# Attention core on TensorE: transposes, scores and values pinned in written order, with lags of six and nine steps instead of five and eight

## The chip, the cores and the metric

The kernel runs on one core of a Trainium2 chip. The metric is the device time of one execution in microseconds (us). The kernel before was timed in three runs; its median is 1542.38 us.

## The reference, cut to what matters

The program is one step of a two-layer trunk over 128 context tokens and 512 latent tokens, width 1024. Layer 0 is a convolution beside an mLSTM, layer 1 is grouped-query attention; each is followed by a SwiGLU feed-forward (FFN). The change lies in layer 1, in the attention of the latent tokens: 8 query heads of width 128, 2 key/value heads, 640 keys (512 latent and 128 cached).

```python
q, k, v = qkv_proj(h, w_in, qg, kg)          # per-head RMSNorm of q and k
q, k = rope_2d(q), rope_2d(k)
k_all = jnp.concatenate([k, k_ctx], axis=1)  # 512 + 128 keys
v_all = jnp.concatenate([v, v_ctx], axis=1)
o = blocked_attention(q, k_all, v_all)       # softmax(q k^T * scale) v, per head
return o @ w_out
```

The 128 context tokens attend only to themselves, in a small computation of their own.

## The kernel before, in words

**Arithmetic.** A product of high precision is made of three matmuls in a rounded float32 form. Each operand is split into a high and a low part, and `mm3` (line 200) issues high×high (line 204), high×low (205) and low×high (206). The splits are made on ScalarE (high part), and on VectorE or GpSimd (low part): line 112 and 115 for weights, 510 and 511 for results (`split_to`).

**Order of the work.** The program is traced by Python in the order in which it is written, and a scheduler then chooses each engine's order: it runs a simulation of the program, and where the next instruction in written order isn't ready there, a later one that is ready goes first. What it chose is fixed in the program; on the chip each engine works through its own list. `issue_after` and `keep_in_program_order` add an edge that the scheduler must respect: the second puts an instruction behind the one that was traced just before it on the same engine. It orders two instructions of one engine and waits for nothing else.

**The attention core.** `attn_layer` (1375) projects keys and values, then queries in two halves (`qc` 0 and 1, five token blocks each, `proj_B`). The core is a generator, `core` (1551), of numbered steps g. Step g works on head g // 5. For g % 5 in 0 to 3 it scores one block of 128 queries against 640 keys (`score`, 1503): two times three matmuls of 320 columns into a pair of PSUM banks (`p2`, two of them), then on VectorE a maximum over the row (1514) and its scaling (1515), on ScalarE the exponential with its sum (1517), on VectorE the reciprocal (1519), on GpSimd the normalisation (1520). The fourth block's result lies in a tile "t", the others in a tile "pw".

A number of steps TL later, step g transposes one block of 128 keys of a head's four probability blocks (`trans`, 1522; TensorE, line 1525, four transposes into one PSUM bank `p1`, of which there are four). The result is copied to a tile "h" as high part (ScalarE, 1532; for the fourth key block VectorE, 1530) and low part (VectorE, 1534). A number of steps VL later, `value` (1536) multiplies it with the values into one more `p1` bank, held over the head's five key blocks: three matmuls of 512 columns (1545 to 1547), or for the cached block one float32 product that runs as two matmuls (1543). After the fifth, `split_to` writes the head's output into H2.

Within a step the written order is transposes, scores, values, and in some steps the transposes of late query blocks (`put_q`, 1451, line 1454) or a piece of the context's attention (`context`, 1466, lines 1470, 1483, 1488).

Nine steps are taken between the blocks of the second query projection. The rest follow in `attn_layer`'s last loop, which hands H2 to `out_proj` (527) ten steps ahead of the end; `out_proj` issues 18 matmuls of heads 0 to 5 ahead of each of the next four steps, takes the remaining steps in a row, and goes on with heads 6 and 7 and the other output tiles.

Of the kernel before, what the change touches and what calls it, by code (L numbers as in the profile page):

```python
# [13 lines left out]
P = 128  # L14
# [32 lines left out]
class Kern:  # L47
# [149 lines left out]
    def p2(self):  # L197
        return self.psp.tile([P, 2, 512], F32, tag="p2", name="p2", bufs=self.pairs)

    def mm3(self, out, w, x, first, last):  # L200

        t = self.nc.tensor
        with self.behind(self.then):
            t.matmul(out, w[0], x[0], start=first, stop=False)  # L204
        t.matmul(out, w[0], x[1], start=False, stop=False)  # L205
        t.matmul(out, w[1], x[0], start=False, stop=last)  # L206

# [1167 lines left out]
    def attn_layer(self, H, mods):  # L1375


        nc, I = self.nc, self.I
# [5 lines left out]
        V, Vl = [self.ht(FR)[:, :1024].rearrange("p (k n) -> p k n", k=4) for _ in range(2)]  # L1384
# [26 lines left out]
        V4 = [self.st()[:, :P] for _ in range(2)]  # L1411
# [49 lines left out]
        def rcol(hq, t, i):  # L1461
            o = 4 * t + hq % 4
            return rk[:, hq // 4, i, o:o + 1]


        def context(kv):
            p = self.p1()
            for i in range(4):
                hq = kv * 4 + i
                nc.tensor.matmul(p[:, i * P:(i + 1) * P], qT[hq // 2][:, hq % 2, 0:P], kTc[:, kv],  # L1470
                                 start=True, stop=True)
            mx, sm, Pm = self.col(4), self.col(4), self.tt()[:, :512].rearrange("p (h n) -> p h n", h=4)
            nc.vector.tensor_reduce(mx, p.rearrange("p (h n) -> p h n", h=4), AX.X, ALU.max)
            nc.vector.tensor_tensor(mx, mx, rk[:, kv, 1, 0:4], ALU.mult)
            for i in range(4):
                nc.scalar.activation(Pm[:, i], p[:, i * P:(i + 1) * P], AF.Exp, bias=mx[:, i:i + 1],
                                     scale=rcol(kv * 4 + i, 0, 0), accum_out=sm[:, i:i + 1])
            nc.vector.reciprocal(sm, sm)
            nc.gpsimd.tensor_tensor(Pm, Pm, sm.unsqueeze(2).to_broadcast([P, 4, P]), ALU.mult)
            yield  # L1480
            pt = self.p1()
            for i in range(4):
                nc.tensor.transpose(pt[:, i * P:(i + 1) * P], Pm[:, i], self.ident)
            PT = self.tt()[:, :512]
            nc.vector.tensor_copy(PT, pt)
            yield
            po = self.p1()
            nc.tensor.matmul(po, Vc[kv], PT, start=True, stop=True)
            self.split_to(H2[:, kv * 4:kv * 4 + 4, 0, 0:P], H2[:, kv * 4:kv * 4 + 4, 1, 0:P],
                          po.rearrange("p (h n) -> p h n", h=4))  # L1490


        Q, Ps, PT, po = {}, {}, {}, {}
        projected = []

        def query(hq):
            Q[hq] = self.ht(FR)
            src = qT[hq // 2][:, hq % 2, P:TOK]
            hi, lo = Q[hq][:, 0:512], Q[hq][:, 640:1152]
            nc.scalar.activation(hi, src, AF.Copy)  # L1500
            nc.gpsimd.tensor_tensor(lo, src, hi.bitcast(F32), ALU.subtract)

        def score(hq, t):
            kv, q = hq // 4, Q[hq]
            if t == 0:
                w = self.wtile(name="pw")
                Ps[hq] = [w[:, i * TOK:(i + 1) * TOK] for i in range(3)] + [self.tt()[:, :TOK]]
            pa = self.p2()[:, :, :HF]
            for a in range(2):
                self.mm3(pa[:, a], (q[:, t * P:(t + 1) * P], q[:, 640 + t * P:640 + (t + 1) * P]),  # L1510
                         (kT[kv][:, a * HF:(a + 1) * HF], kT[kv][:, TOK + a * HF:TOK + (a + 1) * HF]),
                         True, True)
            mx, sm = self.col(1), self.col(1)
            nc.vector.tensor_reduce(mx, pa, AX.XY, ALU.max)
            nc.vector.tensor_scalar(mx, mx, rcol(hq, t + 1, 1), None, ALU.mult)
            Pm = Ps[hq][t]
            nc.scalar.activation(Pm.rearrange("p (a n) -> p a n", a=2), pa, AF.Exp, bias=mx,
                                 scale=rcol(hq, t + 1, 0), accum_out=sm)
            nc.vector.reciprocal(sm, sm)
            nc.gpsimd.tensor_scalar(Pm, Pm, sm[:, 0:1], 0.0, ALU.mult, ALU.add)  # L1520

        def trans(hq, kt):
            p = self.p1()
            for t in range(4):
                nc.tensor.transpose(p[:, t * P:(t + 1) * P], Ps[hq][t][:, kt * P:(kt + 1) * P], self.ident)  # L1525
            h = self.ht(F32 if kt == 4 else FR)
            hi, lo = h[:, :512], h[:, 640:1152]
            PT[hq, kt] = hi, lo
            if kt in (3,):
                nc.vector.tensor_copy(hi, p)  # L1530
            else:
                nc.scalar.activation(hi, p, AF.Copy)
            if kt < 4:
                nc.vector.tensor_tensor(lo, p, hi.bitcast(F32), ALU.subtract)

        def value(hq, kt):
            kv = hq // 4
            if kt == 0:
                po[hq] = self.p1()
            sl = slice(kv * P, (kv + 1) * P)  # L1540
            hi, lo = PT.pop((hq, kt))
            if kt == 4:
                nc.tensor.matmul(po[hq], V4[kv], hi, start=(kt == 0), stop=(kt == 4))
            else:
                nc.tensor.matmul(po[hq], V[:, kt, sl], hi, start=(kt == 0), stop=False)  # L1545
                nc.tensor.matmul(po[hq], Vl[:, kt, sl], hi, start=False, stop=False)
                nc.tensor.matmul(po[hq], V[:, kt, sl], lo, start=False, stop=(kt == 4))
            if kt == 4:
                self.split_to(H2[:, hq, 0, P:TOK], H2[:, hq, 1, P:TOK], po.pop(hq))

        def core():
            query(0)
            TL, VL = 5, 8
            for g in range(40 + VL):
                yield g
                if g > 11:
                    self.wcap = 3
                if TL <= g < 40 + TL:
                    trans((g - TL) // 5, (g - TL) % 5)
                hq, t = g // 5, g % 5  # L1560
                if hq < 8:
                    if t < 4:
                        score(hq, t)
                    else:
                        self.tick(1, 10)
                    if t == 2 and hq < 7:
                        query(hq + 1)
                if VL <= g < 40 + VL:
                    value((g - VL) // 5, (g - VL) % 5)
                if projected and late and g % 3 == 2:  # L1570
                    late.pop(0)()
                if g in (8, 18):
                    ctx = context(g // 10)
                if g in (9, 13, 16, 19, 23, 26):
                    next(ctx, None)

        steps = core()
        for qc in range(2):
            if qc == 1:
# [30 lines left out]
            self.wdone(4)  # L1610
        projected.append(1)
        for g in steps:
            if g >= 30 + 8:
                yield H2
        self.wcap = 6
        yield
# [316 lines left out]
```

## Time and profile before

| What | Value |
|---|---|
| Median of 3 runs | 1542.38 us (1541.84 to 1544.18) |
| The profiled execution's own time | 1540.22 us |
| Its span in the trace | 1538.4 us |
| TensorE busy (matmuls) | 1509.1 us, 98% of the span |
| VectorE, ScalarE, GpSimd busy | 905.8, 582.7, 539.9 us |
| Mean granted TensorE clock | 0.998 of full speed |

A row of a timeline gives start, duration, engine, line, operation and tiles, and in brackets the idle time of the engine before it with what ended it. Matmuls are pipelined: the duration of one reaches to its modelled end, and the next may start earlier; what one costs is the distance from its start to the next start. PEld is the load of a matmul's stationary operand.

### The profile page before, as it was taken

To read this page: it belongs to the slowest core of one execution; us is meant where nothing else is said; L and a number is where in the kernel's file an instruction comes from. 1 tells how busy PE (TensorE), PEld (TensorE's weight loads), DVE (VectorE), ACT (ScalarE), POOL (GpSimd) and SP (SyncE) were. 2 spreads that over 40 slices of the span, in tenths; PEclk is the share of its full clock that TensorE was granted. 3 is DMA by queue.
4 is the path that set the end of the run, shared out by engine and by line. 5 is a ranking of instruction groups with operands and counts; after the bars stand their busy time and mean duration, and the time that the engine had idled before them with its cause. 6 is when DMAs were issued, how large, how long until landed. Compare 5 with 4: busy or idle time off the path is not lost.

```text
span 1538.4 us, 24266 instructions
## 1 busy us (share of the span) xinstructions
PE 1509.1 (98%) x9722; PEld 1405.2 (91%) x9722; DVE 905.8 (59%) x1514; ACT 582.7 (38%) x1153; POOL 539.9 (35%) x366
## 2 busy tenths in 40 slices
PE   8899999999999999999999999999999999999998
PEld 7789888899999999999998877899998998989996
DVE  5888633668976773756576588747653333333335
ACT  5666558444212212212135448626431221212123
POOL 3388411232213222222232445423325524344341
PEclk9999999999999999999999999999999999999999
DMA  9323223534534342423353121122321221312121
GB/s 366 125 87 113 93 90 110 189 124 134 181 110 144 112 156 83 137 75 132 101 177 120 42 82 37 42 102 83 118 102 55 83 83 41 110 55 98 67 69 69
DMA packets 63850, 165.36 MB, mean 107 GB/s; under 512 B 6904, under 2 KB 14112, under 8 KB 63738
## 3 DMA queue, kind: packets, MB, share of 16 engines
q1 hardware_dynamic: 63050, 162.90, 31.0%
q8 instruction: 76, 1.25, 0.3%
q10 hardware_dynamic: 688, 0.92, 0.2%
q14 instruction: 36, 0.29, 0.1%
HBM read 157.53 MB, written 6.26 MB: 106 GB/s over the span
## 4 chain that ended last, share of the span: by engine, by line
PE 84%; DVE 6%; DMA 3%; ACT 3%; POOL 1%; issue 1%; SPq 0%; ACTq 0%; DVEq 0%; POOLq 0%
PE p L204 25%; PE p L206 25%; PE p L205 25%; PE p L263 1%; ACT w L112 1%; POOL w L115 1%; PE p L1525 1%; DVE acc L236 1%; DMA raw<-in_wab 1%; DMA raw<-in_wfo 1%; DVE w L115 1%; PE p L1545 1%; DVE h L524 1%; DVE acc L234 1%; POOL t L903 1%
## 5 line engine op out<-in xcount | busy, mean ns | idle before, releaser
L204 PE MATMUL p<-H,w 128*128 128x320 f32 (+1 forms) x1968 | 609.7, 311 | 3.6 <-ACT t L869 2.2
L206 PE MATMUL p<-H,w 128*128 128x320 f32 (+1 forms) x1968 | 608.8, 310 | 0.0
L205 PE MATMUL p<-H,w 128*128 128x320 f32 (+1 forms) x1968 | 607.1, 309 | 0.0
L115 POOL TENSOR_TENSOR w<-raw,w 128x1024 fp32r<-128x1024 f32 x123 | 310.4, 2528 | 729.8 <-ACT w L112 714.4
L204 PEld LDWEIGHTS p<-H,w 128*128 128x128 f32 x1968 | 369.8, 188 | 13.6 <-issue 3.4
L205 PEld LDWEIGHTS p<-H,w 128*128 128x128 f32 x1968 | 370.5, 188 | 0.7 <-issue 0.2
L206 PEld LDWEIGHTS p<-H,w 128*128 128x128 f32 x1968 | 370.0, 188 | 1.3 <-issue 1.1
L112 ACT ACTIVATE w<-raw 128x1024 fp32r<-128x1024 f32 x178 | 186.9, 1057 | 385.2 <-PE p L206 259.0
L236 DVE SCALAR_TENSOR_TENSOR acc<-mraw,cs,acc 128x512 f32<-128x512 f32 x196 | 174.8, 937 | 0.0
L1629 DVE TENSOR_TENSOR t<-t,p 128x320 f32<-128x320 f32 x88 | 42.6, 484 | 178.4 <-ACT t L1628 176.6
L1628 ACT ACTIVATE t<-p 128x320 f32<-128x320 f32 x88 | 38.1, 433 | 215.3 <-PE p L206 215.3
L115 DVE TENSOR_TENSOR w<-raw,w 128x1024 fp32r<-128x1024 f32 x55 | 77.2, 1404 | 63.0 <-ACT w L112 63.0
L204 PE MATMUL p<-h,w 128*128 128x320 f32 x352 | 109.3, 310 | 1.2 <-DVE h L524 1.2
L511 DVE TENSOR_TENSOR h<-t,h 128x320 fp32r<-128x320 f32 x88 | 87.4, 993 | 36.1 <-ACT h L510 36.1
L205 PE MATMUL p<-h,w 128*128 128x320 f32 x352 | 108.6, 309 | 0.0
L206 PE MATMUL p<-h,w 128*128 128x320 f32 x352 | 108.6, 309 | 0.0
L524 DVE SCALAR_TENSOR_TENSOR h<-p,modT,h 128x128 f32<-128x128 f32 (+2 forms) x189 | 75.0, 431 | 56.5 <-PE p L206 56.4
L517 DVE TENSOR_TENSOR t<-p,h 128x512 f32<-128x512 f32 (+1 forms) x61 | 41.4, 681 | 80.8 <-PE p L206 80.2
L205 PE MATMUL p<-w,h 128*128 128x512 f32 (+1 forms) x224 | 87.9, 392 | 0.0
L204 PE MATMUL p<-w,h 128*128 128x512 f32 (+1 forms) x224 | 87.8, 392 | 0.0
L518 POOL TENSOR_TENSOR h<-h,t 128x512 f32<-128x512 f32 x50 | 69.4, 1391 | 52.0 <-DVE t L517 52.0
L206 PE MATMUL p<-w,h 128*128 128x512 f32 (+1 forms) x224 | 87.6, 391 | 0.0
(346 smaller groups left out, 2150.3 us busy)
## 6 DMA issues: line engine op xcount, KB each, us to landing
raw<-in_wfi SPq DMA_DIRECT2D x88, 512.0 KB, 3.5
mraw<-in_wmod SPq DMA_DIRECT2D x160, 256.0 KB, 3.4
raw<-in_wfo SPq DMA_DIRECT2D x44, 512.0 KB, 3.5
raw<-in_wab SPq DMA_DIRECT2D x16, 512.0 KB, 3.5
raw<-in_wc SPq DMA_DIRECT2D x12, 512.0 KB, 3.9
h<-in_xT SPq DMA_DIRECT2D x14, 320.0 KB, 6.1
h<-in_wmod SPq DMA_DIRECT2D x8, 512.0 KB
raw<-in_woab SPq DMA_DIRECT2D x8, 512.0 KB, 3.5
```

The source lines that it names most:

```text
L112: self.hi_last = self.nc.scalar.activation(hi, r, AF.Copy).ins,
L115: e.tensor_tensor(lo, r, hi.bitcast(F32), ALU.subtract)
L204: t.matmul(out, w[0], x[0], start=first, stop=False)
L205: t.matmul(out, w[0], x[1], start=False, stop=False)
L206: t.matmul(out, w[1], x[0], start=False, stop=last)
L236: nc.vector.scalar_tensor_tensor(acc[:, c], w, s, bias if k == 0 else acc[:, c], ALU.mult, ALU.add)
L511: j = self.nc.vector.tensor_tensor(lo, src, hi.bitcast(F32), ALU.subtract)
L517: nc.vector.tensor_tensor(tmp, ps, gate, ALU.mult)
L518: (e or nc.gpsimd).tensor_tensor(x, x, tmp, ALU.add)
L524: self.nc.vector.scalar_tensor_tensor(x, ps[:, b - a * HF:e - a * HF], gate[:, k, c:c + 1], x, ALU.mult, ALU.add)
L1628: nc.scalar.activation(s[:, sl], pg, AF.Silu)
L1629: nc.vector.tensor_tensor(s[:, sl], s[:, sl], pu, ALU.mult)
```

## The change

It adds edges of the kind `keep_in_program_order` to the first matmul of each group of the core: the first of a `score` (its first half alone), the first of the four transposes of a `trans`, the first matmul of a `value`. Transposes come six steps behind the scores (TL 6, it was 5) and values nine (VL 9, it was 8); the core has 49 steps instead of 48, and H2 is handed over at step 39 instead of 38. The start and stop flags in `value` are written as constants of the same value.

```diff
-    def mm3(self, out, w, x, first, last):
+    def mm3(self, out, w, x, first, last, pin=False):
...
         with self.behind(self.then):
-            t.matmul(out, w[0], x[0], start=first, stop=False)
+            i = t.matmul(out, w[0], x[0], start=first, stop=False)
+        if pin:
+            self.tc.keep_in_program_order(i)
         t.matmul(out, w[0], x[1], start=False, stop=False)
...
                 self.mm3(pa[:, a], (q[:, t * P:(t + 1) * P], q[:, 640 + t * P:640 + (t + 1) * P]),
                          (kT[kv][:, a * HF:(a + 1) * HF], kT[kv][:, TOK + a * HF:TOK + (a + 1) * HF]),
-                         True, True)
+                         True, True, a == 0)
...
             for t in range(4):
-                nc.tensor.transpose(p[:, t * P:(t + 1) * P], Ps[hq][t][:, kt * P:(kt + 1) * P], self.ident)
+                i = nc.tensor.transpose(p[:, t * P:(t + 1) * P], Ps[hq][t][:, kt * P:(kt + 1) * P], self.ident)
+                if t == 0:
+                    self.tc.keep_in_program_order(i)
...
             if kt == 4:
-                nc.tensor.matmul(po[hq], V4[kv], hi, start=(kt == 0), stop=(kt == 4))
+                self.tc.keep_in_program_order(nc.tensor.matmul(po[hq], V4[kv], hi, start=False, stop=True))
             else:
-                nc.tensor.matmul(po[hq], V[:, kt, sl], hi, start=(kt == 0), stop=False)
+                self.tc.keep_in_program_order(
+                    nc.tensor.matmul(po[hq], V[:, kt, sl], hi, start=(kt == 0), stop=False))
                 nc.tensor.matmul(po[hq], Vl[:, kt, sl], hi, start=False, stop=False)
-                nc.tensor.matmul(po[hq], V[:, kt, sl], lo, start=False, stop=(kt == 4))
+                nc.tensor.matmul(po[hq], V[:, kt, sl], lo, start=False, stop=False)
...
-            TL, VL = 5, 8
+            TL, VL = 6, 9
...
-            if g >= 30 + 8:
+            if g >= 30 + 9:
                 yield H2
```

## Rows read from the trace of the kernel before

**Rows 1.** The page, part 1: TensorE's busy time over the whole span.
```profile
PE 1509.1 (98%) x9722; PEld 1405.2 (91%) x9722; DVE 905.8 (59%) x1514; ACT 582.7 (38%) x1153; POOL 539.9 (35%) x366
```

**Rows 2.** Windows: core alone, and core's end. Stretch, length, busy us (instructions), clock.
```profile
917.60:994.80 77.20, 74.04 (x449) 61.04 (x448) 65.34 (x143) 59.18 (x126) 38.96 (x41) 1.00 0.07 22
994.80:1016.00 21.20, 21.20 (x141) 20.03 (x139) 5.61 (x13) 5.63 (x10) 6.42 (x5) 1.00 0.48 184
```

**Rows 3.** Groups of instructions by line, TensorE, 917.6 to 994.8 us.
```profile
L1525 PE MATMUL p<-ident,pw 128*128 128x128 f32 x108 | 19.7, 276 | 1.7 <-DVE H L511 0.8 <-DVE h L1534 0.6 <-DVE modT L273 0.3
L204 PE MATMUL p<-h 128*128 128x320 f32 x54 | 18.4, 341 | 0.4 <-ACT pw L1517 0.4
...
L1545 PE MATMUL p<-h 128*128 128x512 f32 x28 | 11.7, 417 | 0.9 <-DVE h L1534 0.9
...
L1525 PE MATMUL p<-ident,t 128*128 128x128 f32 x35 | 8.3, 274 | 0.0
L1543 PE MATMUL p<-h,s 128*128 128x512 f32 x14 | 7.2, 593 | 0.0
```

**Rows 4.** Timeline of all engines, one passage between two heads, 953.8 to 961.5 us.
```profile
953.85 1.02 PE L1543 MATMUL p<-h,s 128*128 128x512 f32 x2
...
954.71 0.38 PE L1525 MATMUL p<-ident,pw 128*128 128x128 f32 x2
...
956.03 0.49 PE L1525 MATMUL p<-ident,pw 128*128 128x128 f32 x3
...
956.36 0.27 PE L1525 MATMUL p<-ident,t 128*128 128x128 f32 x1
...
956.39 0.39 PE L204 MATMUL p<-h 128*128 128x320 f32 x1
...
957.83 0.55 PE L1525 MATMUL p<-ident,pw 128*128 128x128 f32 x3 [0.33 <-DVE H L511]
...
959.16 0.50 PE L1545 MATMUL p<-h 128*128 128x512 f32 x1 [0.67 <-DVE h L1534]
...
959.49 0.40 PE L1546 MATMUL p<-h 128*128 128x512 f32 x1
...
960.42 0.31 PE L204 MATMUL p<-h 128*128 128x320 f32 x1
...
961.14 0.88 ACT L1517 ACTIVATE pw<-p,col,rk 128x640 f32<-128x640 f32 x1 [1.24 <-DVE col L1519]
961.15 0.31 PE L206 MATMUL p<-h 128*128 128x320 f32 x1
```

**Rows 5.** TensorE's waits, 917.6 to 994.8 us: us in total, times, longest.
```profile
PE p L1545 <- DVE h L1534: 0.9, 2, 0.7
PE p L1525 <- DVE H L511: 0.8, 3, 0.3
PE p L1525 <- DVE h L1534: 0.6, 1, 0.6
```

**Rows 6.** Timeline of all engines: the core's last score and its softmax.
```profile
999.15 0.30 PE L204 MATMUL p<-h 128*128 128x320 f32 x1
...
1000.23 0.82 DVE L1514 TENSOR_REDUCE col<-p 128x1 f32<-128x640 f32 x1 [3.80 <-PE p L206]
...
1001.40 0.89 ACT L1517 ACTIVATE t<-p,col,rk 128x640 f32<-128x640 f32 x1 [5.17 <-DVE col L1515]
...
1002.66 0.81 POOL L1520 TENSOR_SCALAR t<-t,col 128x640 f32<-128x640 f32 x1 [4.64 <-DVE col L1519]
```

**Rows 7.** Timeline of all engines: behind the core's last value matmul.
```profile
1016.30 0.60 ACT L510 ACTIVATE H<-p 128x512 fp32r<-128x512 f32 x1 [4.25 <-PE p L1543]
...
1016.93 0.69 DVE L511 TENSOR_TENSOR H<-p,H 128x512 fp32r<-128x512 f32 x1 [5.98 <-ACT H L510]
```

**Rows 8.** Windows ahead of the core, with TensorE's clock. Columns as in rows 2.
```profile
823.20:826.10 2.90, 1.89 (x15) 1.47 (x13) 0.80 (x3) 0.40 (x3) 0.00 (x0) 1.00 0.54 221
826.10:829.80 3.70, 3.70 (x12) 2.88 (x12) 3.50 (x6) 2.50 (x8) 0.00 (x0) 0.54 0.00 0
```

## The prediction

> **What bounds the kernel now.** The first view is the page's list of busy engines: TensorE works 1509.1 of 1538.4 us [rows 1], so no instruction of the other engines is worth anything unless TensorE waits for it. The change adds and removes no matmul, so all it can win is time in which TensorE stands still. The second view is the windows. From 917.6 us (the first transpose) to 994.8 us (the first output matmul) TensorE is busy 74.04 of 77.20 us, behind that to 1016 us it is busy throughout [rows 2]. The reader is to see two things there: the core can still give something, its end can't; and VectorE has 65.34 us of work in the same 77.20, so it is never long ahead of TensorE.
>
> Busy time counts a pipelined matmul to its modelled end, so I weigh the core by starts instead. From the timeline [rows 4]: three transposes from 956.03 to 956.36 us, 0.11 each; five score matmuls from 960.42 to 961.15, 0.146; four value matmuls from 959.49 to 960.42, 0.233; the float32 pair from 953.85 to 954.71, 0.43 each. The groups by line [rows 3] give the counts: 108 + 35 transposes, 3 × 54 score matmuls, 3 × 28 value matmuls, 14 of the pairs' halves. That is 403 of the 449 instructions [rows 2]; the other 46, mostly short ones, I price as transposes. 143 × 0.11 + 162 × 0.146 + 84 × 0.233 + 14 × 0.43 + 46 × 0.11 = 15.7 + 23.7 + 19.6 + 6.0 + 5.1 = 70.1 us. So 7.1 of the 77.2 us are lost, and that is **the most that a better order can win**.
>
> The third view is TensorE's waits in that stretch [rows 5]: values waiting for the low part of the transposed block (0.9 us), transposes waiting for a PSUM bank that the previous head's output holds (0.8) or that an earlier transpose's copy holds (0.6). The timeline shows how they come about [rows 4]: the scheduler let transposes run ahead of the written order, seven in these rows from 956.03 on, with one score between them; the copies lag, the next group waits 0.33 us for a bank, and the values behind it 0.67 us for the copy. These are bunches, not a lack of an engine.
>
> **The change, part by part.**
>
> *Even spacing.* In written order a step is four transposes, six score matmuls, three value matmuls: 0.44 + 0.88 + 0.70 = 2.02 us, or 1.14 without a score. With one group of transposes per step the copy has three steps, over 5 us, until its values, as it had on paper before. I take it that the three waits [rows 5] go: 2.3 us. Each of their 6 occurrences also costs a restart: the waiting matmul at 959.16 hands over after 0.33 us, its like at 959.49 after 0.23, so 0.1 each, 0.6 us. Gain 2.9 us; bounds 0 and 7.1.
>
> *Lag six.* A pin makes everything behind it on TensorE wait, so what matters is whether the data is there. The last score, with VectorE and ScalarE free, starts at 999.15, its normalised block is ready at 1002.66 + 0.81 = 1003.47: 4.32 us [rows 6]. The first transpose group of a head needs the block of its fourth score. With lag six the fourth transpose comes after the rest of the score's step (score 0.88, float32 values 0.86), a step without score (1.14), a whole one (2.02) and three transposes (0.33): 5.23 us, slack 0.91. With lag five it would be 0.88 + 0.70 + 1.14 + 0.33 = 3.05, short by 1.27; so the pin needs the sixth step, and the sixth step is what keeps the pin cheap. But a loaded chain is longer: the score at 956.39 got its exponential done only at 961.14 + 0.88 = 962.02, 5.63 us after its start [rows 4], where the last one needs 1001.40 + 0.89 − 999.15 = 3.14 [rows 6]. With those 2.49 us more the block is ready after 6.81, and TensorE would stand 1.58 us at the head's first transposes. Bounds: 0, and 1.58 at each of 7 heads (the eighth lies under the output matmuls), 11.1 us. The loaded chain was in the very bunch that goes, so I take a value near the low end: one such wait, 1.6 us.
>
> *Score pairs.* A score needs the PSUM pair of the score two before, 2 × 2.02 = 4.04 us earlier; free after 3.14, slack 0.90. What delays one chain delays both, so I count this wait in the one above.
>
> *Lag nine.* Three steps behind the transposes as before, so as many "h" tiles are alive: nothing. The probabilities' tiles live one step longer; a head's are free after the step in which the head after next begins to score, and its transposes are written ahead of that score: nothing, unless the sixth weight slot is taken, and then it is a wait of one exponential for four transposes, 0.44 us.
>
> *The end.* One transpose and value group (1.14 us) moves behind 994.8, where the output matmuls of heads 0 to 5 fill every gap [rows 2]. They aren't pinned, so they can still fill one: nothing. If that cover were gone, the last head's split, 0.60 + 0.69 us [rows 7], would show: +1.3.
>
> *Queues.* No step of the change moves a DMA: the loads of output weights and of x are traced from the same ticks and the same end of the core, and SP's order is not pinned. On GpSimd the normalisations keep their order. The context's pieces and the late query transposes stay at their step numbers; one that is late would now hold the next pinned group, which I leave in the bounds.
>
> Sum: −2.9 + 1.6 = −1.3 us against the profiled span of 1538.4. That execution took 1540.22 us, the median of the runs is 1542.38; I put the same difference on the median: **1541.1 us**, 1538.5 to 1545 with its own uncertainty. A measurement of this kernel can tell about 0.2%, 3.1 us, from no change; so this is no change.
>
> **Rivals.**
>
> *The order pays more.* The 7.1 us are all due to bunching and 5 of them go: 1537.4. For it: only 77.20 − 74.04 = 3.2 us of them are idle time in the profile [rows 2], the rest lies in short gaps that a busy TensorE hides. Against: VectorE's 65.34 of 77.20 us leaves little room for an even beat.
>
> *Slower: the pin at each head's first transposes.* The normalised fourth block comes later than 5.23 us after its score in most heads; scores and values behind it can't pass any more, whereas before the scheduler put others first. Five of seven heads at 1.58 us are 7.9, less the 2.9: +5.0, **1547.4**. It decides as soon as the chain is over 0.91 us longer than the free one; one weight split on ScalarE or GpSimd ahead of the block is enough. For it: the loaded chain above. Against: that chain had a bunch ahead of it.
>
> *The clock falls.* Ahead of the core, TensorE is busy 1.89 of 2.90 us with little in it, and in the 3.70 us that follow the granted clock is 0.54, close to its level of 1.2 GHz [rows 8]: 3.70 × 0.46 = 1.7 us lost. In the core the clock stayed at 1.00 through all its waits [rows 2]. If the pins gather the waits into one longer stop per head, 8 × 1.7 = 13.6 us: 1556. The Trainium skill (TensorE: Matmul & The Clock Gate, "A second HAM failure mode: psum-queue depth-cycling") says that small idle times between groups of matmuls, as PSUM banks are cycled, are enough to make the clock swing; by that rule the sum would be this one, and the core as it was, with six such idle times at full clock, does not bear it out.
>
> *It does not do what it says.* Only first matmuls are pinned; transposes two to four and the second half of a score may still float, and the order may come out much as before. Then what is left is the longer lag: within 1 us of 1542.
>
> **How the numbers follow.** Forecast 0.42, of which 0.03 reach below −3.1 us and 0.03 above +3.1; the change without effect 0.04; the larger gain 0.30; the pin that waits 0.21; the clock 0.03. Faster 0.30 + 0.03 = 0.33, same 0.36 + 0.04 = 0.40, slower 0.21 + 0.03 + 0.03 = 0.27. The range takes in the larger gain down to 1535.5 (the ceiling of 7.1 us lies at 1535.3) and the waiting pin up to 1548.5; outside are the clock, the worst of the waits (up to 11.1 us), and gains from other stages that a new order brings by chance.
>
> **What would show it.** Right: from the first transpose to the first output matmul about 76 us instead of 77.2; no wait of values for the low part; transposes waiting, if at all, for a normalised block from GpSimd, in one or two heads; clock 1.00. Wrong: a wait of transposes for line 1520, or of scores for line 1517, in nearly every head; a new wait at the end of the core; the core's length unchanged but another stage longer or shorter; or an order on TensorE that still puts two groups of transposes in a row.

## The result and the profile after

The changed kernel takes **1548.66 us** (median of 6 runs, 1544.71 to 1549.83), the kernel before 1542.11 beside it (6 runs, 1539.74 to 1544.18): a ratio of 1.0040 [1.0025, 1.0054], some 6.5 us slower. The forecast was 1541.1 us and no change; the time also lies just outside its range, which ended at 1548.5.

The profiled execution took 1549.27 us, its span 1547.5, 9.1 more than before. The page's first part answers to [rows 1]:

```profile
PE 1513.8 (98%) x9722; PEld 1409.1 (91%) x9722; DVE 905.6 (59%) x1514; ACT 584.0 (38%) x1153; POOL 538.9 (35%) x366
```

The counts of instructions are the same on every engine, and TensorE is busy 4.7 us longer with the same 9722 matmuls: they ran partly at a lower clock. To see where, I compare stretches with the same work in both. The instructions of each engine stand in the same order up to the core's first transposes and again behind the core, and SP's order is the same throughout, so three stretches tell all: up to the core's first score matmul, from there to the 150th output matmul (all of the core and what fills its end), and the rest. The timelines of TensorE, first before, then after, give their ends:

```profile
900.84 0.39 PE L204 MATMUL p<-h 128*128 128x320 f32 x1
...
1023.29 0.31 PE L206 MATMUL p<-H,w 128*128 128x320 f32 x1
```
```profile
904.29 0.39 PE L204 MATMUL p<-h 128*128 128x320 f32 x1
...
1032.54 0.31 PE L208 MATMUL p<-H,w 128*128 128x320 f32 x1
```

The middle stretch took 1023.29 − 900.84 = 122.45 us and now takes 1032.54 − 904.29 = 128.25, which is 5.8 more. In a second execution of each program it was 122.44 and 128.42, 6.0 more. On the mean of the two it is 122.4 and 128.3: **5.9 us more in the core**. This stretch repeats to 0.2 us and serves as the measure below. Another 3.4 us lie ahead of the core, where nothing was changed; that part differs from one execution to the next (the last section), and behind the core the two are alike within 0.2.

TensorE's waits in the middle stretch, before and then after, each line an operation, what it waited for, us in total, times, longest:

```profile
PE p L204 <- ACT pw L1517: 1.0, 2, 0.6
PE p L1545 <- DVE h L1534: 0.9, 2, 0.7
PE p L1525 <- DVE H L511: 0.8, 3, 0.3
PE p L1525 <- DVE h L1534: 0.6, 1, 0.6
PE p L1525 <- DVE modT L273: 0.3, 1, 0.3
PE p L1454 <- DVE H L511: 0.2, 1, 0.2
```
```profile
PE p L204 <- ACT pw L1519: 5.7, 4, 3.6
PE p L1527 <- POOL t L1522: 1.7, 2, 1.1
PE p L1550 <- DVE h L1538: 0.4, 1, 0.4
PE p L1527 <- DVE H L513: 0.4, 1, 0.4
```

3.7 us of waits became 8.1 (summed before rounding). The bunches of [rows 5] shrank to 0.8 us, as meant, and the transposes wait for the normalised block from GpSimd (now line 1522) in two heads only. But the score matmuls wait 5.7 us for exponentials, 3.6 of them in one place. Windows of the changed kernel around it, columns as in [rows 2]:

```profile
917.00:923.50 6.50, 6.50 (x40) 5.74 (x39) 5.31 (x11) 4.54 (x9) 3.74 (x6) 1.00 0.00 0
923.50:927.40 3.90, 0.35 (x4) 0.11 (x2) 3.58 (x10) 3.87 (x8) 2.92 (x5) 1.00 0.00 0
927.40:931.50 4.10, 4.01 (x19) 3.97 (x20) 1.95 (x5) 1.74 (x5) 1.93 (x2) 0.58 0.00 0
...
937.00:1001.50 64.50, 60.58 (x361) 49.16 (x361) 53.15 (x119) 48.40 (x104) 30.90 (x32) 1.00 0.10 34
```

TensorE does almost nothing for 3.9 us while ScalarE is busy for 3.87 of them, and in the next 4.10 us its clock is 0.58: 4.10 × 0.42 = 1.7 us more. 8.1 − 3.7 of waits and 1.7 of clock are 6.1 us, against 5.8 measured in this execution. What ScalarE does there stands in its timeline, with TensorE's rows that begin and end the stop:

```profile
920.98 0.39 PE L204 MATMUL p<-h 128*128 128x320 f32 x1
...
922.05 1.28 ACT L1611 ACT_TABLE_LOAD   x1
923.35 0.31 ACT L1611 ACTIVATE rk<-rk,eps 128x20 f32<-128x20 f32 x1
923.56 1.06 ACT L1536 ACTIVATE h<-p 128x512 fp32r<-128x512 f32 x2
...
924.51 0.63 ACT L1502 ACTIVATE h<-h 128x512 fp32r<-128x512 f32 x1
...
925.16 1.28 ACT L1519 ACT_TABLE_LOAD   x1
926.46 0.88 ACT L1519 ACTIVATE pw<-p,col,rk 128x640 f32<-128x640 f32 x1
...
927.49 0.63 PE L204 MATMUL p<-h 128*128 128x320 f32 x1 [3.63 <-ACT pw L1519]
```

This is step 7, head 1's third score. It needs the PSUM pair of head 1's first score (920.98), and that pair is free when its exponential is done, at 926.46 + 0.88 = 927.34: 6.36 us. Ahead of that exponential ScalarE takes the square root for the norm of heads 4 to 7's queries (line 1611), which is traced when the core's steps have begun. It needs another table than the exponential, so one table is loaded for it and one behind it, 1.28 us each.

The same chain is in the kernel before:

```profile
917.78 0.39 PE L204 MATMUL p<-h 128*128 128x320 f32 x1
...
918.63 1.28 ACT L1606 ACT_TABLE_LOAD   x1
...
921.71 1.28 ACT L1517 ACT_TABLE_LOAD   x1
...
923.00 0.89 ACT L1517 ACTIVATE pw<-p,col,rk 128x640 f32<-128x640 f32 x1
...
924.03 0.42 PE L204 MATMUL p<-h 128*128 128x320 f32 x1
```

It took 923.89 − 917.78 = 6.11 us, about as long, and TensorE hardly waited. A window over the two loads shows it busy 4.21 of 4.40 us:

```profile
918.60:923.00 4.40, 4.21 (x31) 3.68 (x30) 4.09 (x10) 4.34 (x7) 1.71 (x4) 1.00 0.00 0
```

Between head 1's second and third score it ran eight transposes, eight value matmuls and four query transposes. The eight value matmuls are written for steps 8 to 10; the free order had pulled them ahead of the score of step 7. In the changed kernel only four transposes stand between these two scores, and no values.

### The profile page after: what moved, and what is told of

Its sections match the earlier page's. It is cut to its first block, busy times and chain, and to the rows that moved or that the text cites. A ratio compares the mean times of both kernels' runs of the same rounds, so it can differ in the third digit from the quotient of the medians.

```text
span 1547.5 us, 24265 instructions
## 1 busy us (share of the span) xinstructions
PE 1513.8 (98%) x9722; PEld 1409.1 (91%) x9722; DVE 905.6 (59%) x1514; ACT 584.0 (38%) x1153; POOL 538.9 (35%) x366
## 4 chain that ended last, share of the span: by engine, by line
PE 69%; DVE 6%; ACT 3%; issue 1%; DMA 1%; POOL 0%; ACTq 0%; DVEq 0%
PE p L204 22%; PE p L208 22%; PE p L207 22%; DVE acc L238 1%; PE p L1527 1%; DMA raw<-in_wfo 1%; DVE t L405 0%; DVE h L526 0%; PE p L1547 0%; ACT pw L1519 0%; DVE H L513 0%; DVE acc L236 0%; ACT w L112 0%; POOL w L115 0%; PE p L1552 0%
## 5 line engine op out<-in xcount | busy, mean ns | idle before, releaser
L238 DVE SCALAR_TENSOR_TENSOR acc<-mraw,cs,acc 128x512 f32<-128x512 f32 x196 | 179.2, 959 | 0.0
```

The costliest lines, as they stand in the source:

```text
L238: nc.vector.scalar_tensor_tensor(acc[:, c], w, s, bias if k == 0 else acc[:, c], ALU.mult, ALU.add)
```

## The experiments

All times are medians; "core" is the stretch from the first score to the 150th output matmul, "waits" TensorE's waits in it, both of the profiled execution; "lags" are the steps of transposes and values behind scores. The ratio is taken over all runs and not from the two medians.

| kernel | lags | pins | us (before beside it) | ratio [95%] | core | waits |
|---|---|---|---|---|---|---|
| before_again | 5/8 | none | 1541.13 (1542.93) | 0.9991 [0.9980, 1.0002] | 122.4 | 3.7 |
| after_again | 6/9 | all | 1547.86 (1542.93) | 1.0029 [1.0016, 1.0043] | 128.4 | 8.1 |
| lag_alone | 6/9 | none | 1546.31 (1542.93) | 1.0024 [1.0013, 1.0036] | 127.1 | 7.9 |
| pins_alone | 5/8 | all | 1557.27 (1542.93) | 1.0093 [1.0077, 1.0110] | 137.6 | 14.4 |
| after_no_sqrt | 6/9 | all | 1543.22 (1541.66) | 1.0012 [1.0000, 1.0024] | 124.4 | 5.4 |
| before_no_sqrt | 5/8 | none | 1547.21 (1541.66) | 1.0035 [1.0025, 1.0045] | 127.5 | 7.1 |
| pins_from_12 | 6/9 | steps 12 on | 1546.50 (1541.66) | 1.0022 [1.0008, 1.0036] | 126.5 | 5.9 |
| lag_late | 5/8, then 6/9 | none | 1544.56 (1541.66) | 1.0016 [1.0001, 1.0031] | 124.9 | 6.3 |
| late_both | 5/8, then 6/9 | steps 12 on | 1543.11 (1541.63) | 1.0021 [1.0008, 1.0034] | 124.5 | 4.9 |
| late10_both | 5/8 for two heads | steps 12 on | 1549.60 (1541.63) | 1.0058 [1.0044, 1.0072] | 128.3 | 6.7 |
| pins_to_11 | 6/9 | steps 0 to 11 | 1548.16 (1541.63) | 1.0038 [1.0023, 1.0054] | 127.7 | 8.3 |
| fill_wait | 6/9 | all | 1545.44 (1541.96) | 1.0028 [1.0016, 1.0041] | 125.7 | 4.2 |
| before_fill | 5/8 | none | 1541.38 (1542.76) | 0.9994 [0.9982, 1.0006] | 122.7 | 3.9 |

**The two kernels again**, unchanged. 

> The kernel before, unchanged, timed against itself as a control. Every theory expects a ratio of 1.000 within 0.2%. It tells how far two executions of one program differ ahead of the core: the order of instructions up to the core's first transpose is the same in both kernels on every engine, yet the changed kernel's trace reached it 3.4 us later. If that is spread, the start of the first transpose differs by 2 to 4 us between the profiles of one program too.

> The changed kernel, unchanged, beside the same runs of the kernel before. Expected 1.004 again, with the one long wait of TensorE (about 3.6 us, a score of head 1 for the exponential two scores before it) in the trace again. If the wait is missing while the time is the same, the wait is not the cause.

The core repeats to 0.2 us in both, and the stop of 3.6 us is there again. The first score starts 1.6 us apart in the two profiles of the kernel before and 0.8 apart in those of the changed one. That is less than the 2 to 4 expected; over all profiles the spread is wider (the last section).

**Each half of the change alone.** The longer lags without pins, as an edit of the kernel before:

```diff
-            TL, VL = 5, 8
+            TL, VL = 6, 9
...
-            if g >= 30 + 8:
+            if g >= 30 + 9:
```

> Only the lags: six and nine, no pins. If the pins are the cost (theory A), TensorE's order stays free, the 3.6 us wait is filled by other work and the time is 1539 to 1543 us. If the longer lag is the cost (theory B: one more step to drain, tiles held longer), the time is that of the changed kernel, 1546 to 1549 us.

The core takes 127.1 us, 4.7 of the 5.9: **most of the loss comes with the longer lag, without any pin**. The stop is there too; windows of this kernel:

```profile
921.00:924.00 3.00, 0.92 (x7) 0.44 (x5) 2.92 (x8) 2.97 (x6) 2.16 (x4) 1.00 0.00 0
924.00:928.50 4.50, 4.49 (x19) 4.00 (x20) 2.71 (x6) 1.97 (x5) 1.96 (x2) 0.66 0.01 4
```

It is shorter (1.9 us), since the scheduler puts more transposes ahead of the score, but the clock falls all the same. And the pins with the old lags:

```diff
-            TL, VL = 6, 9
+            TL, VL = 5, 8
...
-            if g >= 30 + 9:
+            if g >= 30 + 8:
```

> Only the pins, with lags five and eight. Theory A: by the prediction's budget each head's first transposes are asked for 1.27 us before their block can be ready, so 7 x 1.3 = 9 us more than the changed kernel's other waits of about 4: 1552 to 1558 us, with TensorE waiting for GpSimd's normalisation in nearly every head. Theory B: the lag was the cost, so 1541 to 1544 us.

The time lies where the first theory put it. With lag five the pinned transposes wait 11 times for GpSimd's normalised blocks, and the stop at step 7 is there too, 3.0 us long:

```profile
PE p L1527 <- POOL t L1522: 6.6, 7, 1.7
PE p L204 <- ACT pw L1519: 4.9, 5, 3.0
PE p L1527 <- POOL pw L1522: 2.3, 4, 0.9
```

So pins need the sixth step, as the prediction had it. And the stop doesn't need the longer lag: in written order even lag five puts only four transposes between these two scores. Either half of the change alone uncovers the passage, the lag under a free order and the pins at the old lags.

**The table loads taken out.** after_no_sqrt and before_no_sqrt leave out the square root in the norm of heads 4 to 7's queries; VectorE scales the mean instead, and no table is changed there.

```diff
-            nc.scalar.activation(ms, ms, AF.Sqrt, bias=self.eps, scale=1.0 / P)
+            if qc == 0:
+                nc.scalar.activation(ms, ms, AF.Sqrt, bias=self.eps, scale=1.0 / P)
+            else:
+                nc.vector.tensor_scalar(ms, ms, 1.0 / P, EPS, ALU.mult, ALU.add)
```

> The changed kernel without the square root in the norm of the second query half (heads 4 to 7 get another scale; everything else stays), so that ScalarE loads no other function table between the scores. Theory A' (the loss is one passage: TensorE stands behind a score whose exponential is queued behind two table loads, and the clock falls behind it): the 3.6 us wait shrinks to under 1 and the 1.7 us of the clock go, 1542.5 to 1544.5 us. Rival (the pins lose in many small waits at the heads): 1547 us and more, the long wait replaced by others.

> The same omission in the kernel before. Theory A': there the two table loads lie under transposes and values of head 0, so leaving them out is worth 0 to 1 us: 1541.5 to 1543 us. If it wins 4 us or more here too, the table loads cost both kernels alike and don't explain the difference.

In the changed kernel the core falls from 128.3 to 124.4 us, with clock 1.00 from its start to its end:

```profile
PE p L204 <- ACT pw L1519: 2.9, 4, 1.6
PE p L1527 <- POOL t L1522: 1.1, 1, 1.1
```

The wait at step 7 falls from 3.63 to 1.55 us, not to under 1 as expected, and no lower clock follows it: 2.1 + 1.7 = 3.8 us, which is nearly all of the difference. So 3.9 of the 5.9 us are the one ScalarE passage with its two loads. In the kernel before, the same edit missed what was expected: its core became 5.0 us longer. Without pins the scheduler wrote another order, with a new wait of values for a transpose's copy and a low clock behind it:

```profile
939.93 0.79 PE L1545 MATMUL p<-h 128*128 128x512 f32 x1 [2.58 <-DVE h L1534]
```
```profile
938.00:942.00 4.00, 2.07 (x5) 1.69 (x6) 3.97 (x9) 2.64 (x6) 1.92 (x2) 0.68 0.37 131
```

So this run tells nothing of what the loads cost there; it shows that one stop that a free order happens to make, with the others beside it, costs nearly as much as the whole change.

**Where in the core pins and lags matter.** Pins only from step 12, lags 6/9; and its opposite, pins only up to step 11 (`g < 12`):

```diff
+        on = [False]
...
-                if t == 0:
+                if t == 0 and on[0]:
                     self.tc.keep_in_program_order(i)
...
+                on[0] = g >= 12
```

> Lags six and nine throughout, pins only from step 12 on. Theory A': the passage with the table loads lies in steps 6 to 9 and its loss comes with the longer lag, pinned or not, so it begins as with the lags alone (a wait of about 1.9 us and a lowered clock): 1545 to 1547.5 us. Rival (the pins in the first steps are the cost): 1541 to 1543 us.

> The other half: lags six and nine, pins only in steps 0 to 11. By difference to the run with pins from step 12 (126.7 us to the 150th output matmul) and to the changed kernel (128.4), the pins of the first steps cost 1.7 us: 128 to 129.5 us there, the 3.6 us wait and the lowered clock behind it as in the changed kernel, 1546 to 1549 us in all. If the long wait needs the later pins too, it is gone here.

126.5 against lag_alone's 127.1: pins in the later heads win 0.6 us at most. The core takes 127.7 with pins at the start alone, half a microsecond more than without and a little under the 128 to 129.5 expected, and the stop is 3.6 us long as in the changed kernel. The two don't add up: 127.1 − 0.6 + 0.5 is 127.0, and the changed kernel takes 128.3. So a difference of about one microsecond between two such orders can't be put down to one edit. Then head 0 keeps lags 5/8, which puts its transposes and values back into the passage; without pins, and with pins from step 12:

```diff
+            at = lambda lag: {i + lag - (i < 5): i for i in range(40)}
+            ts, vs = at(TL), at(VL)
...
-                if TL <= g < 40 + TL:
-                    trans((g - TL) // 5, (g - TL) % 5)
+                if g in ts:
+                    trans(ts[g] // 5, ts[g] % 5)
...
-                if VL <= g < 40 + VL:
-                    value((g - VL) // 5, (g - VL) % 5)
+                if g in vs:
+                    value(vs[g] // 5, vs[g] % 5)
```

> No pins; head 0's transposes and values keep lags five and eight, the other heads have six and nine. Theory A': the passage with the table loads is covered as in the kernel before, no stop and no lowered clock there: 1541 to 1544 us. Rival (the longer lag costs at every head, by PSUM banks held longer): 1545 to 1547 us, as with the lags alone.

> Head 0 with lags five and eight, unpinned; from head 1 on lags six and nine, pins from step 12. From the first score to the 150th output matmul the kernel before took 122.6 us, the changed one 128.4, late lags without pins 125.0. If pins in even steps win what the prediction gave them (2.9 us of waits less 1.6), this is 123.5 to 124 us there and 1541 to 1544 us in all. If, as pins from step 12 against lags alone say (126.7 against 127.3), pins with long lags are worth next to nothing, it is 124 to 125 us there and 1543 to 1545.

Both cover the passage (no wait of over 0.2 us there, clock 1.00 throughout) and save 2.3 and 2.0 us against lag_alone and pins_from_12. Both stay above before, by 2.4 and 2.1; the time of lag_late lies between what its two theories expected. What these two microseconds are isn't shown. They may be the longer lag in the later heads, or the new order of the whole core. The longest waits, of lag_late and then of late_both:

```profile
PE p L1545 <- DVE h L1534: 1.9, 4, 0.7
PE p L1483 <- POOL t L1479: 1.5, 1, 1.5
```
```profile
PE p L204 <- ACT pw L1521: 3.1, 6, 0.9
PE p L1529 <- POOL t L1524: 1.6, 3, 1.1
```

Without pins it is values that wait for copies, and a piece of the context's attention that waits for GpSimd; with pins it is scores that wait for a pair. The two kernels have no common cause in view. Keeping 5/8 for two heads (`i < 10`) instead of one:

> As the run before, but heads 0 and 1 have lags five and eight; only from head 2 on six and nine with pins from step 12. Theory A' (the first 12 steps decide, by what there is to do under the table loads): the first score of head 2 comes 39.5 us after the first score, as in the kernel before (43.3 in the changed one, 40.4 with late lags), and the whole is within 2 us of the kernel before, 1540.5 to 1543.5. If the step that is left out between lag five and six costs wherever it stands, 1543 to 1545.

Neither time came: the core takes as long as in the changed kernel. Where the lags change over, a transpose waits 3.4 us for a copy at 939.39, and from 930 to 950 us the clock is 0.83. Why the order stops there wasn't tested.

**The clock by itself.** fill_wait is the changed kernel with 30 transposes of the identity into a bank that nobody reads, pinned at step 7 where TensorE stops:

```diff
+                if g == 7:
+                    idle = self.p1()
+                    for _ in range(30):
+                        self.tc.keep_in_program_order(
+                            nc.tensor.transpose(idle[:, :P], self.ident, self.ident))
```

> The changed kernel with 30 idle transposes (of the unit matrix, into a PSUM bank of their own, read by nobody) pinned on TensorE behind head 0's second transposes, that is into the 3.6 us wait. They add about 30 x 0.11 = 3.3 us of TensorE work. If the lowered clock behind the wait comes from TensorE having had next to nothing to do, and costs 1.7 us, the granted clock stays at 1.00 behind it and the kernel is faster for the added work: 126.5 to 127.3 us from the first score to the 150th output matmul (128.4 in the changed kernel), 1545 to 1547.5 us in all. If the clock falls for another reason, or its price is already hidden, 128 to 129 us there and 1548 to 1550.

TensorE now reaches the score at 924.38 with a wait of 0.35 us left, and this window of the passage shows no lower clock:

```profile
920.00:930.00 10.00, 8.96 (x72) 8.38 (x70) 7.91 (x19) 7.27 (x15) 5.69 (x8) 1.00 0.01 2
```

The core takes 125.7 us, less than the 126.5 expected: **30 × 0.11 = 3.3 us of useless work make it 2.6 us shorter.** 1.7 of that is the clock. The stop itself was only filled; other waits shrank too, 4.2 + 3.3 = 7.5 us against 8.1. The last 0.3 I can't place. Taken over all profiles, a stop of 1.9 us or more at step 7 had a lower clock behind it in six of six, and the nine without such a stop had none there. In the whole time the gain can't be told from the spread (1.0028 here, 1.0029 for after_again).

before_fill puts 12 such transposes into the passage of [rows 8], far ahead of the core, in the kernel before:

```diff
+            idle = self.p1() if (gi, a) == (2, 1) else None
+            self.idle(idle, 5)
...
+            self.idle(idle, 7)
```

> The kernel before with 12 idle transposes (of the unit matrix, read by nobody) in the norm ahead of the key projection, five ahead of its first and seven ahead of its second group of TensorE instructions, where TensorE is busy 1.9 of 2.9 us and the granted clock is 0.54 over the next 3.7 us. If the fall is the price of having little to do, and 1.7 us, the clock stays at 1.00 there and the stretch from 819 us to the first score is 1 to 2 us shorter; the whole 1539 to 1541.5 us, at the edge of what five rounds can tell. If the clock falls all the same, or the transposes hold up the norm, the stretch is as long as before or longer by up to 1 us.

```profile
820.00:825.00 5.00, 5.00 (x28) 4.24 (x28) 4.79 (x10) 1.14 (x4) 0.00 (x0) 1.00 0.48 182
825.00:830.00 5.00, 5.00 (x33) 4.26 (x32) 2.81 (x6) 1.64 (x8) 0.00 (x0) 1.00 0.24 99
```

The fall of [rows 8] isn't in this profile, and the stretch from a matmul ahead of it (at 819.21 us in the kernel before) to the first score is 80.1 us instead of 81.6, although the idle work is in it. But one profile doesn't show that the filling did it. The other fourteen profiles have the same instructions in the same order up to the first score. Eleven have the fall here, and three have none without any filling (the changed kernel's own, after_no_sqrt and late_both), with the same two waits of TensorE ahead of it. The changed kernel's window over the passage, and that of the kernel before:

```profile
815.00:835.00 20.00, 19.00 (x111) 17.04 (x110) 17.60 (x35) 11.75 (x30) 0.87 (x1) 1.00 0.27 106
```
```profile
815.00:835.00 20.00, 18.99 (x93) 16.01 (x93) 16.96 (x34) 12.46 (x28) 1.45 (x2) 0.91 0.32 119
```

Without the fall the stretch takes 80.3 us, with it 81.6 to 81.7. So these profiles measure what a fall costs here, 1.4 us, and leave open whether filling prevents it in this place. By the whole time before_fill can't be told from no change, so no version here is shown to beat the kernel before.

## Why the prediction was wrong

- **What bounds the kernel**: right. TensorE's waits, with the lower clock behind one of them, account for the result.
- **Even spacing**: the mechanism was right, the size too large. Of the 2.3 us of copy and bank waits 0.8 are left, so 1.5 went, and not 2.9. And a free order gets nearly the same: pins in the later heads win 0.6 us at most.
- **Lag six, GpSimd's block**: right in size, 1.7 us in two heads where 1.6 was put. The rival of a pin that waits in five of seven heads did not come; its time, 1547.4, was near the result by another cause. It is what pins_alone shows at lag five.
- **Score pairs**: this step failed. It took the pair as free 3.14 us after its score, from the undisturbed last score [rows 6], found 0.90 us of slack, and counted the wait into that of the transposes. Its own loaded chain of 5.63 us, set against the 4.04 between two such scores, would already have made a wait of 1.59, and [rows 3] show scores waiting 0.4 us for exponentials. In the changed kernel the scores' waits are a second item, 5.7 us against 1.7. At step 7 the chain takes 6.36 us, since ScalarE loads two tables ahead of it. The rows for it were in the trace of before, where the chain took 6.11: I priced the chain in an undisturbed place and between two later heads, and not in the passage where the second query projection's norm meets the first heads. after_no_sqrt shows that passage as 3.9 us of the 5.9. The Trainium skill (ScalarE: Activation LUTs, "Table sets: the hidden batching unit") says that an exponential and a square root need different sets, at about 5.3 us for two loads; the trace agrees on the loads and not on the price, 2 × 1.28 = 2.56 us.
- **Lag nine "nothing", lag six only as slack**: the other half of the failure. A longer lag isn't only more time for the chain of a head; at the core's start it takes away the work that covers other chains. In before, head 0's transposes and values lie exactly under the table loads. lag_alone, with no pin at all, loses 4.7 us; of that lag_late gives back 2.3. A pin takes the same cover away by holding to the written order, as pins_alone shows at lag five; the prediction left that out too.
- **The clock**: the price of 1.7 us a fall was about right, the place wrong. It was put at every head or nowhere; it came once, behind the stop. fill_wait shows this fall to hang on the stop: filled, it is gone. The rule of the Trainium skill quoted in the prediction (TensorE: Matmul & The Clock Gate, "A second HAM failure mode: psum-queue depth-cycling") is not borne out in the changed kernel: from 937.0 to 1001.5 us it has six waits of 0.36 to 1.10 us, three of them for a PSUM bank, at clock 1.00. In pins_alone one fall did come behind short waits alone (the last section).
- **The end, queues**: right. Transposes and values of the last head fill the output matmuls as before, behind the core both kernels agree within 0.2 us, and SP's order is the same.

That the stop is as long as it is because of the table loads is shown by leaving them out. That the lag uncovers it under a free order is shown by lag_alone, and by lag_late, where head 0 has the old lags and no stop; that pins uncover it too is shown by pins_alone. Where the last 2.1 to 2.4 us of lag_late and late_both come from stays open: their waits differ, and no run tried a third PSUM pair.

## What to carry to other kernels

Look for slack in the busiest passage of the chain, not in its cleanest: a second stage that shares ScalarE with the first steps of a loop, above all one that changes the activation table, can double the time until a buffer comes free. A longer software lag takes work away from the start of the loop, and so does an order that is held to the written one; before either, list which instructions there cover which chain. And where a stop of the bounding engine can't be removed, price it with the lower clock behind it.

## What the hardware showed beyond that

A fall of the clock cost the same wherever it came, 1.7 us by the granted clock: in the changed kernel's core (4.10 × 0.42), in lag_alone (924 to 929 us, 5.00 × 0.34) and in [rows 8]. In the core a fall followed each stop of 1.9 (twice), 3.0 and 3.6 us at step 7, and single waits of 2.6 and 3.4 elsewhere. Waits of up to 1.7 us standing alone left the clock at 1.00, and so did one of 2.1 in lag_alone. But short waits close together could bring a fall: in pins_alone the clock fell behind waits of 0.33, 0.39 and 0.99 us, with TensorE busy 2.30 of 4.00 us ahead of the fall:

```profile
943.00:947.00 4.00, 2.30 (x12) 1.43 (x13) 2.40 (x7) 1.58 (x4) 1.79 (x3) 1.00 0.04 14
947.00:950.50 3.50, 3.50 (x15) 3.10 (x14) 1.73 (x3) 0.60 (x1) 0.00 (x0) 0.51 0.00 0
```

And falls also come where TensorE never waits. In the changed kernel, far ahead of the core, with no wait of TensorE from 140 to 200 us:

```profile
165.00:170.00 5.00, 5.00 (x21) 4.24 (x21) 2.58 (x5) 4.18 (x15) 4.90 (x3) 0.66 0.11 25
...
195.00:200.00 5.00, 5.00 (x32) 5.00 (x32) 1.68 (x4) 3.42 (x13) 0.00 (x0) 0.81 0.00 0
```

The kernel before, with the same instructions in the same order, has clock 1.00 from 150 to 200 us in its profiled execution, and a fall near 220 in its second one. How many falls there are ahead of the core, and where, differs between executions. In the fourteen profiles with the same instructions up to the first score, the clock lost there is zero to four times 1.7 us. The score starts at 898.4 us in the one with none (after_no_sqrt), at 900.8 to 901.1 with one and at 903.5 to 905.1 with four. That is most of the spread ahead of the core, and it is why differences of one or two microseconds here are read from a stretch and not from the whole time. What sets these falls off stays open.
